# A second copy that writes over its source tile, weight sums in three instructions, and PSUM tiles of two banks in a two-layer encoder

## The chip, the cores and the metric

The kernel runs on one core of one Trainium2 chip. The metric is device microseconds of one execution. Three runs of the kernel before took 2028.54, 2030.12 and 2031.21 us, median 2030.12 us. Engines are called as the profile calls them: PE (matrix products), PEld (its weight loads), DVE (vector engine), ACT (scalar engine), POOL and SP (SP issues most DMAs).

## The reference

A two-layer encoder over 256 tokens of width 2048, all in float32. Layer 0 mixes tokens by chunked spatial gating, layer 1 by grouped-query attention; both also attend to 256 memory tokens. Each layer ends with a SwiGLU feed-forward, the part that the change touches most (`D_FF` is 5632).

```python
def swiglu(h, w_gate_up, w_down):
    gate, up = jnp.split(h @ w_gate_up, 2, axis=-1)
    return (jax.nn.silu(gate) * up) @ w_down

def reference(x, mem, g_mix, g_ffn, w_in_a, g_v_a, w_spatial, b_spatial, w_in_b, g_q_b, g_k_b,
              g_mem, w_mem_kv, g_mq, g_mk, w_out, w_gate_up, w_down):
    for l in range(DEPTH):
        h = rms_norm(x, g_mix[l])
        if l % N_MIXERS == 0:
            z = h @ w_in_a[ia]
            tok_in, q_mem = jnp.split(z, [2 * TOK_WIDTH], axis=-1)
            tok_out = chunked_spatial_gating(tok_in, g_v_a[ia], w_spatial[ia], b_spatial[ia])
        else:
            z = h @ w_in_b[ib]
            tok_in, q_mem = jnp.split(z, [TOK_WIDTH + 2 * KV_WIDTH], axis=-1)
            tok_out = gqa_axial_attention(tok_in, g_q_b[ib], g_k_b[ib], cos, sin)
        mem_out = memory_attention(q_mem, mem, g_mem[l], w_mem_kv[l], g_mq[l], g_mk[l])
        x = x + jnp.concatenate([tok_out, mem_out], axis=-1) @ w_out[l]
        x = x + swiglu(rms_norm(x, g_ffn[l]), w_gate_up[l], w_down[l])
    return x
```

(Lines that set indices and tables are left out.)

## The kernel before, in words

**Products.** A float32 operand is split into `hi` (rounded to the PE's fp32r type by ACT) and `lo` (the rest, by DVE). A product is three matmuls, hi·hi, lo·hi and hi·lo (`matmul3`, L197 to L201). Tokens stand on two partition blocks t = 0, 1 of 128 rows. Weights come by SP's DMAs into `raw` tiles of four 128x512 blocks; `halves` (L263) makes `whi` on ACT (L269) and `wlo` on DVE (L270), each in a ring of three buffers (`W_TILES`).

**The feed-forward.** Eleven gate/up blocks f of 512 columns go in three chunks (0 to 3, 4 to 7, 8 to 10). For each f a `Pair` (L325) computes a gate block and an up block for both t; `Silu` and a multiply give the activation `a` (L803 to L805, a ring `sg` of two buffers). Behind each chunk two `Pair`s (jj = 0, 1 in the code) multiply the chunk's activations with `w_down` and add into the residual tiles `X`. A `Pair` walks over items i, each two 128-row blocks of the weights. Slow items (`eight`) are 8 products, 24 matmuls, into four PSUM banks named 2, 3, 4, 8 (pool `psa`, printed as `acc`). Fast items (`seven`) are a seven-product scheme, 21 matmuls: sums of weight blocks (`T`, L361 to L365), sums of activations (`activation_sums`), the outer products 2, 3, 4 in `acc` banks and four inner products 1, 5, 6, 7 in banks of the pool `psm` (printed as `m`, four tiles of one bank). After the last fast item `inner` (L409) combines the four inner banks into four `e` tiles; in the down projection these are then added into X (L420); `outer` (L428) adds the outer banks at the end of the Pair.

**Turning the activations.** The down projection needs the activations with features on partitions. `turned` (L207) does it in steps: ACT copies the 16-bit planes of `a` apart into a tile `planes` (L212), a DMA on ACT's queue turns them into `back` (L213), and ACT copies them together again (L216), in the kernel before into the tile of `planes`. Then `split_a` (L785) splits the result: hi by ACT (L193), lo by DVE (L194); for two f of chunks 0 and 1 it makes the activation sums too.

**Buffers.** All these tiles (planes, back, hi, lo, sums) come from `big()` (L76): one tag `a` in the stage's pool `room["p"]`, with 26 buffers in a feed-forward stage (`FFN_TILES`) and 36 in a mixing stage. A tile's buffer is free when its last reader is done; an instruction that writes a new tile waits for a free buffer.

**What sets the order.** The program emits work in ticks: `later(n, f)` runs f when n more half-items have been emitted. The order of the instructions on each engine is then made by a planner (`schedule_with_timeline_sim=True`, L863), which simulates the program and takes, on each engine, the earliest emitted instruction that its simulation holds ready; an instruction that waits for a buffer in the simulation is passed over. On the chip each engine runs its list in order. How many `a` tiles live at once in a chunk's down projection follows from `fast` and `quick` (each listed item keeps a hi and a lo tile of activation sums, those of `fast` until the layer's last gate/up Pair) and from `split_a` (a hi and a lo tile for each f and t, kept for the chunk):

```python
FFN_TILES = 26
...
        fast = (0, 1, 2)
...
            quick = [2 * f + 1 for f in chunk[:2 if chunk[-1] < 10 else l]]
...
                    later(3 + t if f == chunk[-1] else 12 + t, lambda a=a, t=t, f=f: turn_a(a, t, f))
```

Of the kernel before, what the change touches and what calls it, by code (L numbers as in the profile page):

```python
# [17 lines left out]
P = 128  # L18
# [36 lines left out]
def encoder(ctx: ExitStack, tc: tile.TileContext, x, mem, g_mix, g_ffn, w_in_a, g_v_a, w_spatial, b_spatial,  # L55
# [11 lines left out]
    psm = ctx.enter_context(tc.tile_pool(name="psm", bufs=4, space=PS))  # L67
# [13 lines left out]

    def misc():
        return psm.tile([P, NB], F32, tag="m", name=nm("m"))
# [37 lines left out]
    X = [[xp.tile([P, NB], F32, name=f"x_{t}_{j}") for j in range(4)] for t in range(NT)]  # L121
# [10 lines left out]
    def gain_columns(kind):  # L132
        gcol[kind] = const.tile([P, 32], F32, name=f"gcol_{kind}")
        gps = misc()
# [72 lines left out]
    def turned(src, ticks, then):  # L207
# [7 lines left out]
        def finish():  # L215
            nc.scalar.copy(planes.rearrange("p (n h) -> p n h", h=2), back.rearrange("p (h n) -> p n h", h=2))  # L216
            then(a)
# [106 lines left out]

    class Pair:  # L325
# [5 lines left out]
        def __init__(self, parts, sums, w, na, nb, order, fast, into=None):  # L331
            self.parts, self.sums, self.w, self.na, self.nb, self.into = parts, sums, w, na, nb, into
            self.bank, self.part, self.ready = {}, {}, {}
# [20 lines left out]
        def prepare(self, i):  # L354
# [5 lines left out]
            if i in self.fast:  # L360
                T = room["p"].tile([P, KC3, NB], F32, tag="T", name=nm("T"), bufs=2)  # L361
                nc.vector.tensor_tensor(raw[:, 0], raw[:, 0], raw[:, 1], ALU.add)  # L362
                nc.vector.tensor_tensor(T[:, 0], raw[:, 0], raw[:, 3], ALU.add)
                nc.vector.tensor_tensor(T[:, 1], T[:, 0], raw[:, 1], ALU.subtract)
                nc.vector.tensor_tensor(T[:, 2], T[:, 0], raw[:, 2], ALU.add)  # L365
                self.ready[i] = raw, T
# [15 lines left out]
        def seven(self, i, raw, T):  # L382
            t1, w00, w10, w11 = halves(raw, KC4)
            t2, t3, t4 = halves(T, KC3)
# [23 lines left out]
        def inner(self):  # L408

            b, o = self.bank, self.into  # L410
            e, v, f, y = [room["p"].tile([P, NB], F32, tag=f"e{i}", name=nm("e"), bufs=1) for i in range(4)]
# [455 lines left out]
```

## Time and profile before

| | |
|---|---|
| median of three runs | 2030.12 us (2028.54 to 2031.21) |
| the profiled execution's own time | 2030.63 us |
| its span, first to last instruction | 2028.8 us, so 1.8 us lie around it |
| granted PE clock over the span | 0.998 |
| PE busy | 2006.1 us, 99% |
| PEld / DVE / ACT busy | 82% / 79% / 60% |
| first matmul, last matmul's end, from the span's start | 4.7 us, 2024.3 us |

How to read it: the page gives busy time by engine, then the chain of work that ended last, then groups of instructions by source line with the mean duration and the idle time in front of them. A timeline row is start, duration, engine, line, operation, output<-inputs, form, count, and in brackets how long the engine had been idle and which instruction ended the wait. A row of a stretch gives its length, then busy time and the number of instructions in brackets for each engine, then the granted PE clock, the DMA share and GB/s. Matmuls are pipelined: each is shown 0.39 us long, but the next one starts after about 0.23 us, so time that PE lost is read from counts of matmuls and not from its busy time.

### The profile page before, as it was taken

To read this page: it belongs to the slowest core of one execution; us is meant where nothing else is said; L and a number is where in the kernel's file an instruction comes from. 1 tells how busy PE (TensorE), PEld (TensorE's weight loads), DVE (VectorE), ACT (ScalarE), POOL (GpSimd) and SP (SyncE) were. 2 spreads that over 40 slices of the span, in tenths; PEclk is the share of its full clock that TensorE was granted. 3 is DMA by queue.
4 is the path that set the end of the run, shared out by engine and by line. 5 is a ranking of instruction groups with operands and counts; after the bars stand their busy time and mean duration, and the time that the engine had idled before them with its cause. 6 is when DMAs were issued, how large, how long until landed. Compare 5 with 4: busy or idle time off the path is not lost.

```text
span 2028.8 us, 24312 instructions
## 1 busy us (share of the span) xinstructions
PE 2006.1 (99%) x9058; PEld 1656.6 (82%) x9058; DVE 1603.5 (79%) x1862; ACT 1213.8 (60%) x1509; POOL 50.5 (2%) x80
## 2 busy tenths in 40 slices
PE   8999999999999999999999999999999999999999
PEld 7888888888788887888888888888887888878887
DVE  5576558998889988798666886599987899878977
ACT  7765476666445664456756765756654467634662
POOL 2010000000000000000010100000000000000000
PEclk9999999999999999999999999999999999999999
DMA  9754575666656666577766444756765566755564
GB/s 331 246 183 150 184 218 170 233 198 209 212 184 234 191 214 206 188 231 220 227 203 207 157 144 145 218 187 206 239 218 187 186 203 219 226 188 202 193 212 145
DMA packets 265791, 411.79 MB, mean 203 GB/s; under 512 B 74428, under 2 KB 74792, under 8 KB 265672
## 3 DMA queue, kind: packets, MB, share of 16 engines
q1 hardware_dynamic: 198800, 385.79, 56.3%
q10 hardware_dynamic: 64824, 18.02, 4.8%
q0 software_dynamic: 2048, 6.42, 1.0%
q8 instruction: 71, 1.16, 0.2%
q14 instruction: 48, 0.39, 0.1%
HBM read 390.26 MB, written 4.19 MB: 194 GB/s over the span
## 4 chain that ended last, share of the span: by engine, by line
PE 92%; DVE 3%; DMA 3%; ACT 1%; issue 1%; SPq 0%; DVEq 0%; ACTq 0%
PE acc L201 26%; PE acc L200 26%; PE acc L199 26%; PE m L201 4%; PE m L199 4%; PE m L200 4%; DMA a<-a 2%; DVE wlo L270 2%; ACT whi L269 1%; PE m L205 1%; PE m L515 0%; DMA x<-in_x 0%; PE m L661 0%; DVE T L365 0%; DMA raw<-in_w_in_a 0%
## 5 line engine op out<-in xcount | busy, mean ns | idle before, releaser
L270 DVE TENSOR_TENSOR wlo<-raw,whi 128x2048 fp32r<-128x2048 f32 (+2 forms) x465 | 839.0, 1826 | 242.8 <-ACT whi L269 235.8
L269 ACT CAST whi<-raw 128x2048 fp32r<-128x2048 f32 (+2 forms) x465 | 702.1, 1537 | 459.7 <-PE acc L200 376.5
L199 PE MATMUL acc<-whi,h 128*128 128x512 f32 x1440 | 562.6, 391 | 0.4 <-ACT whi L269 0.4
L200 PE MATMUL acc<-whi,h 128*128 128x512 f32 x1440 | 561.9, 390 | 0.0
L201 PE MATMUL acc<-wlo,h 128*128 128x512 f32 x1440 | 518.2, 391 | 0.8 <-DVE wlo L270 0.8
L199 PE MATMUL acc<-whi,a 128*128 128x512 f32 x1062 | 413.8, 392 | 2.5 <-DVE x L428 1.4
L200 PE MATMUL acc<-whi,a 128*128 128x512 f32 x1062 | 415.6, 391 | 0.0
L201 PE MATMUL acc<-wlo,a 128*128 128x512 f32 x1062 | 400.6, 391 | 0.8 <-DVE wlo L270 0.8
L201 PEld LDWEIGHTS acc<-wlo,h 128*128 128x128 f32 x1440 | 270.6, 188 | 56.9 <-DVE wlo L270 1.4
L199 PEld LDWEIGHTS acc<-whi,h 128*128 128x128 f32 x1440 | 270.6, 188 | 55.5 <-ACT whi L269 0.8
L200 PEld LDWEIGHTS acc<-whi,h 128*128 128x128 f32 x1440 | 270.6, 188 | 55.4
L199 PEld LDWEIGHTS acc<-whi,a 128*128 128x128 f32 x1062 | 199.7, 188 | 46.5 <-DVE x L428 3.0
L201 PEld LDWEIGHTS acc<-wlo,a 128*128 128x128 f32 x1062 | 200.2, 188 | 43.9 <-DVE wlo L270 2.7
L200 PEld LDWEIGHTS acc<-whi,a 128*128 128x128 f32 x1062 | 200.3, 189 | 41.3 <-DVE a L194 0.6
L269 ACT CAST whi<-T 128x1536 fp32r<-128x1536 f32 x82 | 121.4, 1481 | 132.9 <-PE acc L200 99.1
L270 DVE TENSOR_TENSOR wlo<-T,whi 128x1536 fp32r<-128x1536 f32 x82 | 143.9, 1755 | 20.7 <-ACT whi L269 20.7
L199 PE MATMUL m<-whi,a 128*128 128x512 f32 x264 | 103.5, 392 | 5.7 <-ACT whi L269 5.7
L200 PE MATMUL m<-whi,a 128*128 128x512 f32 x264 | 102.8, 390 | 0.0
L216 ACT COPY a<-a 128x1024 uint16<-128x1024 uint16 x60 | 70.2, 1170 | 37.3 <-DMA a<-a 37.1
L201 PE MATMUL m<-wlo,a 128*128 128x512 f32 x264 | 88.7, 395 | 2.4 <-DVE wlo L270 2.4
L362 DVE TENSOR_TENSOR raw<-raw 128x512 f32<-128x512 f32 x82 | 56.5, 688 | 22.8 <-DMA raw<-in_w_gate_up 22.8
L199 PEld LDWEIGHTS m<-whi,a 128*128 128x128 f32 x264 | 49.6, 188 | 18.4 <-ACT whi L269 8.3
(131 smaller groups left out, 1520.0 us busy)
## 6 DMA issues: line engine op xcount, KB each, us to landing
raw<-in_w_gate_up SPq DMA_DIRECT2D x352, 512.0 KB, 4.4
raw<-in_w_down SPq DMA_DIRECT2D x176, 512.0 KB, 5.1
raw<-in_w_out SPq DMA_DIRECT2D x32, 1024.0 KB, 5.2
raw<-in_w_in_a SPq DMA_DIRECT2D x24, 1024.0 KB, 5.1
raw<-in_w_in_b SPq DMA_DIRECT2D x24, 1024.0 KB, 5.0
raw<-in_w_mem_kv SPq DMA_DIRECT2D x16, 1024.0 KB, 5.0
raw<-in_w_in_a SPq DMA_DIRECT2D x7, 512.0 KB, 6.1
x<-in_x SPq DMA_DIRECT2D x8, 256.0 KB, 5.7
```

The source lines that it names most:

```text
L199: nc.tensor.matmul(out, lhsT=a[0], rhs=b[0], start=start, stop=False)
L200: nc.tensor.matmul(out, lhsT=a[1], rhs=b[0], start=False, stop=False)
L201: nc.tensor.matmul(out, lhsT=a[0], rhs=b[1], start=False, stop=stop)
L205: nc.tensor.transpose(dst[:, c * P:(c + 1) * P], src[:, c * P:(c + 1) * P], ident)
L216: nc.scalar.copy(planes.rearrange("p (n h) -> p n h", h=2), back.rearrange("p (h n) -> p n h", h=2))
L269: nc.scalar.copy(hi[:, cut], raw[:, cut])
L270: nc.vector.tensor_tensor(lo[:, cut], raw[:, cut], hi[:, cut].bitcast(F32), ALU.subtract)
L362: nc.vector.tensor_tensor(raw[:, 0], raw[:, 0], raw[:, 1], ALU.add)
```

## The change

Three edits, and what goes with them:

- `turned` gets a flag `over`, set for the feed-forward's activations: the second copy (L216) writes the joined words into the source tile (`sg`) instead of the tile of `planes`, and `split_a` reads them there.
- The weight sums of a fast item are three DVE instructions instead of four, one of them 128x1024; the first two results change places (`raw[:, 0]` and `T[:, 0]`), and with them which product reads which tile.
- The inner banks become two PSUM tiles of two banks, (1, 6) and (5, 7), from a pool that is opened for each stage (`open_rooms`). `inner` then takes three DVE instructions instead of four, and the addition into X three instead of four, with the four `e` tiles made one and X stored in tiles of two blocks. In a fast item that is not a Pair's first, product 6 moves to the front group and product 5 to the rear group. A lone `misc()` tile in a feed-forward stage takes a two-bank tile.

```diff
-    psm = ctx.enter_context(tc.tile_pool(name="psm", bufs=4, space=PS))
+    def open_rooms(scope, name, tiles, banks):
+
+        room["p"] = scope.enter_context(tc.tile_pool(name=name, bufs=tiles, reuse_waits="tile"))
+        room["m"] = scope.enter_context(tc.tile_pool(name=f"ps_{name}", bufs=4 // banks, space=PS))
+        room["banks"] = banks
+
+    def banks2():
+        return room["m"].tile([P, 2, NB], F32, tag="m", name=nm("m"))
+
     def misc():
-        return psm.tile([P, NB], F32, tag="m", name=nm("m"))
+        if room["banks"] == 2:
+            return banks2()[:, 0]
+        return room["m"].tile([P, NB], F32, tag="m", name=nm("m"))
...
-    def turned(src, ticks, then):
+    def turned(src, ticks, then, over=False):
...
         def finish():
-            nc.scalar.copy(planes.rearrange("p (n h) -> p n h", h=2), back.rearrange("p (h n) -> p n h", h=2))
-            then(a)
+            words = src.rearrange("p (c n) -> p c n", c=4) if over else a
+            halves = (src.bitcast(U16) if over else planes).rearrange("p (n h) -> p n h", h=2)
+            nc.scalar.copy(halves, back.rearrange("p (h n) -> p n h", h=2))
+            then(words)
...
-                nc.vector.tensor_tensor(raw[:, 0], raw[:, 0], raw[:, 1], ALU.add)
-                nc.vector.tensor_tensor(T[:, 0], raw[:, 0], raw[:, 3], ALU.add)
-                nc.vector.tensor_tensor(T[:, 1], T[:, 0], raw[:, 1], ALU.subtract)
-                nc.vector.tensor_tensor(T[:, 2], T[:, 0], raw[:, 2], ALU.add)
+                w01 = raw[:, 0].unsqueeze(1).to_broadcast([P, 2, NB])
+                nc.vector.tensor_tensor(T[:, :2], raw[:, 1:4:2], w01, ALU.add)
+                nc.vector.tensor_tensor(raw[:, 0], T[:, 0], raw[:, 3], ALU.add)
+                nc.vector.tensor_tensor(T[:, 2], raw[:, 0], raw[:, 2], ALU.add)
...
-                self.bank[name] = misc() if name in (1, 5, 6, 7) else psa.tile([P, NB], F32, tag="acc", name=nm("acc"))
-                self.part[name] = 0
+                if name in (1, 5, 6, 7):
+                    both = (1, 6) if name in (1, 6) else (5, 7)
+                    self.two[both] = banks2()
+                    self.bank.update({one: self.two[both][:, i] for i, one in enumerate(both)})
+                else:
+                    self.bank[name] = psa.tile([P, NB], F32, tag="acc", name=nm("acc"))
...
-            inner = [(1, get(k0, 0), w00), (5, q5, t1), (6, s2, t2), (7, q7, t3)]
+            inner = [(1, get(k0, 0), w00), (6, s2, t2), (5, q5, t1), (7, q7, t3)]
             outer = [(2, get(k1, 0), w10), (3, q3, w11), (4, get(k1, 1), t4)]
             if self.bank:
-                inner, outer = inner[:1] + outer[:2], inner[1:] + outer[2:]
+                inner, outer = inner[:2] + outer[:2], inner[2:] + outer[2:]
...
-            nc.scalar.copy(e, b[1])
-            nc.vector.tensor_tensor(v, b[6], e, ALU.subtract)
-            nc.vector.tensor_tensor(f, b[5], v, ALU.add)
-            nc.vector.tensor_tensor(v, b[7], v, ALU.add)
-            nc.vector.tensor_tensor(y, b[7], f, ALU.add)
+            nc.scalar.copy(E[:, 0], b[1])
+            nc.vector.tensor_tensor(E[:, 3], b[6], E[:, 0], ALU.subtract)
+            nc.vector.tensor_tensor(E[:, 1:3], self.two[5, 7], E[:, 3:].to_broadcast([P, 2, NB]), ALU.add)
+            nc.vector.tensor_tensor(E[:, 3], b[5], E[:, 2], ALU.add)
...
+            if t:
+                nc.vector.tensor_tensor(o[0], o[0], E[:, 2], ALU.subtract)
+                nc.vector.tensor_tensor(o[1], o[1], E[:, 3], ALU.add)
+            else:
+                nc.vector.tensor_tensor(o.whole, o.whole, E[:, :2], ALU.add)
...
-                turned(a, 2, lambda whole: split_a(whole, t, f, aT, aS, half, quick))
+                turned(a, 2, lambda whole: split_a(whole, t, f, aT, aS, half, quick), True)
```

More of the change, by code (lines that the diff above doesn't have):

```diff
@@ L119, in encoder @@
     nc.gpsimd.memset(mhalf, -0.5)
-    X = [[xp.tile([P, NB], F32, name=f"x_{t}_{j}") for j in range(4)] for t in range(NT)]
+    X2 = [[xp.tile([P, 2, NB], F32, name=f"x_{t}_{i}") for i in range(2)] for t in range(NT)]
+    X = [[X2[t][j // 2][:, j % 2] for j in range(4)] for t in range(NT)]
     def load_x(t, j):
@@ L133, in gain_columns @@
         gcol[kind] = const.tile([P, 32], F32, name=f"gcol_{kind}")
-        gps = misc()
+        gps = misc() if room else psa.tile([P, NB], F32, tag="acc", name=nm("acc"))
         nc.tensor.transpose(gps[:, :32], gst[kind], ident[:32, :32])
@@ L323, in activation_sums, with __init__ @@
         return [(hi[:, i, :], lo[:, i, :]) for i in range(4)]
+    class Columns(list):
+        def __init__(self, whole):
+            self.whole = whole
+            super().__init__(whole[:, n] for n in range(2))
     class Pair:
@@ L332, in __init__ @@
             self.parts, self.sums, self.w, self.na, self.nb, self.into = parts, sums, w, na, nb, into
-            self.bank, self.part, self.ready = {}, {}, {}
+            self.bank, self.two, self.part, self.ready = {}, {}, {}, {}
             self.order, self.fast = order, fast
@@ L408, in inner, with add_inner @@
         def inner(self):
-            b, o = self.bank, self.into
-            e, v, f, y = [room["p"].tile([P, NB], F32, tag=f"e{i}", name=nm("e"), bufs=1) for i in range(4)]
-            nc.scalar.copy(e, b[1])
-            nc.vector.tensor_tensor(v, b[6], e, ALU.subtract)
-            nc.vector.tensor_tensor(f, b[5], v, ALU.add)
-            nc.vector.tensor_tensor(v, b[7], v, ALU.add)
-            nc.vector.tensor_tensor(y, b[7], f, ALU.add)
-            if o:
-                for (t, n), x, op in (((0, 0), e, ALU.add), ((0, 1), f, ALU.add), ((1, 0), v, ALU.subtract),
-                                      ((1, 1), y, ALU.add)):
-                    later(1 + 2 * t + n, lambda o=o[t][n], x=x, op=op: nc.vector.tensor_tensor(o, o, x, op))
-            self.out = o or [[e, f], [v, y]]
+            b = self.bank
+            E = room["p"].tile([P, 4, NB], F32, tag="e", name=nm("e"), bufs=1)
+            nc.scalar.copy(E[:, 0], b[1])
+            nc.vector.tensor_tensor(E[:, 3], b[6], E[:, 0], ALU.subtract)
+            nc.vector.tensor_tensor(E[:, 1:3], self.two[5, 7], E[:, 3:].to_broadcast([P, 2, NB]), ALU.add)
+            nc.vector.tensor_tensor(E[:, 3], b[5], E[:, 2], ALU.add)
+            if self.into:
+                for t in range(NT):
+                    later(1 + t, lambda t=t: self.add_inner(E, t))
+            self.out = self.into or [[E[:, 2 * t + n] for n in range(2)] for t in range(NT)]
+        def add_inner(self, E, t):
+            o = self.into[t]
+            if t:
[3 more added lines that the diff above has]
+                nc.vector.tensor_tensor(o.whole, o.whole, E[:, :2], ALU.add)
         def outer(self, t):
@@ L624, in encoder @@
         scope = ExitStack()
-        room["p"] = scope.enter_context(tc.tile_pool(name=f"mix{l}", bufs=MIX_TILES, reuse_waits="tile"))
+        open_rooms(scope, f"mix{l}", MIX_TILES, 1)
         cat = Parts()
@@ L754, in encoder @@
             add_residual(linear(cat, w_out[l], j * NB, units), j, norm, gslice("ffn", l), hF, j < 3)
-        room.pop("p")
+        room.clear()
         scope.close()
         scope = ExitStack()
-        room["p"] = scope.enter_context(tc.tile_pool(name=f"ffn{l}", bufs=FFN_TILES, reuse_waits="tile"))
+        open_rooms(scope, f"ffn{l}", FFN_TILES, 2)
         sums = {}
@@ L814, in encoder @@
                     order.insert(2 * n + (2 if last else 0), i)
-                into = [[X[t][2 * jj + n] for n in range(2)] for t in range(NT)]
+                into = [Columns(X2[t][jj]) for t in range(NT)]
                 pairs.append(Pair(aT, aS, w_down[l], 2 * jj * NB, (2 * jj + 1) * NB, order, quick, into))
@@ L830, in encoder @@
         norm = next_norm
-        room.pop("p")
+        room.clear()
         scope.close()
```

5 lines of the change are left out of this document (3 added, 2 removed).

## The prediction

> **What bounds the kernel now.** I read the page first, then stretches of the trace, then the order of instructions in the stretches where PE lost time.
>
> ```profile
> span 2028.8 us, 24312 instructions
> ...
> PE 2006.1 (99%) x9058; PEld 1656.6 (82%) x9058; DVE 1603.5 (79%) x1862; ACT 1213.8 (60%) x1509; POOL 50.5 (2%) x80
> ...
> PE 92%; DVE 3%; DMA 3%; ACT 1%; issue 1%; SPq 0%; DVEq 0%; ACTq 0%
> ```
>
> PE is the bound: 92% of the chain that ends last is PE. No edit removes a matmul, so a gain can only come from time in which PE lacks work. DVE work that is saved elsewhere is worth nothing. The next rows are stretches of the trace: length, PE busy time with the number of matmuls, the other engines, the granted PE clock. The last four rows list PE alone.
>
> ```profile
> 410.00:480.00 70.00, 70.00 (x310) 57.83 (x309) 64.58 (x62) 47.91 (x39) 0.00 (x0) 1.00 0.71 228
> 526.00:536.00 10.00, 7.88 (x31) 5.34 (x31) 4.67 (x6) 1.93 (x2) 0.00 (x0) 1.00 0.31 108
> 780.00:790.00 10.00, 7.44 (x30) 5.01 (x29) 5.45 (x7) 1.47 (x1) 0.00 (x0) 1.00 0.37 124
> 1529.00:1540.00 11.00, 9.07 (x31) 6.45 (x30) 3.70 (x5) 2.54 (x2) 0.00 (x0) 0.84 0.28 95
> 1784.00:1796.00 12.00, 9.49 (x33) 6.77 (x32) 4.70 (x6) 2.53 (x2) 0.00 (x0) 0.86 0.27 89
> ...
> 495.00:526.00 31.00, 30.32 (x133) 1.00 0.77 246
> 750.00:780.00 30.00, 29.73 (x130) 1.00 0.79 247
> 1498.00:1529.00 31.00, 30.24 (x133) 1.00 0.75 239
> 1755.00:1784.00 29.00, 28.81 (x126) 1.00 0.76 247
> ```
>
> The first row is gate/up work: 70 us for 310 matmuls, 0.226 us each, PE never idle although DVE is busy 92% of it. At that pace the four short stretches lose 10 - 31 x 0.226 = 3.0, 10 - 30 x 0.226 = 3.2, 11 - 31 x 0.226 = 4.0 and 12 - 33 x 0.226 = 4.5 us: 14.7 us. (Counts include about one matmul that straddles the edge, so the true loss is up to 0.2 us larger in each.) The four rows ahead of them lose 0.9, 0.6, 0.9 and 0.5 us: 3.0 us. All eight lie in the down projections of chunks 0 and 1 of both layers. Two knots, an early and a late one, come four times.
>
> **The late knot.** The timeline of the first one:
>
> ```profile
> 505.38 0.68 DVE L194 TENSOR_TENSOR a<-a,a 128x512 fp32r<-128x512 f32 x1
> ...
> 508.54 0.63 ACT L193 CAST a<-a 128x512 fp32r<-128x512 f32 x1
> ...
> 529.24 1.47 ACT L269 CAST whi<-T 128x1536 fp32r<-128x1536 f32 x1 [7.14 <-PE acc L200]
> 530.75 1.76 DVE L270 TENSOR_TENSOR wlo<-T,whi 128x1536 fp32r<-128x1536 f32 x1 [2.43 <-ACT whi L269]
> 530.77 0.50 PE L199 MATMUL m<-whi,a 128*128 128x512 f32 x1 [1.33 <-ACT whi L269]
> 532.42 0.69 DVE L194 TENSOR_TENSOR a<-a,a 128x512 fp32r<-128x512 f32 x1
> 532.56 0.73 PE L201 MATMUL m<-wlo,a 128*128 128x512 f32 x2 [0.60 <-DVE wlo L270]
> ...
> 787.18 0.68 DVE L194 TENSOR_TENSOR a<-a,a 128x512 fp32r<-128x512 f32 x1
> ...
> 1534.44 0.68 DVE L194 TENSOR_TENSOR a<-a,a 128x512 fp32r<-128x512 f32 x1
> ...
> 1790.45 0.69 DVE L194 TENSOR_TENSOR a<-a,a 128x512 fp32r<-128x512 f32 x1
> ```
>
> L193 and L194 are hi and lo of the chunk's last activation, t = 0 first (L194 at 505.38) and then t = 1. For t = 1 hi is made at 508.54 but lo only at 532.42, 24 us later, behind the `wlo` of the next Pair. Without that lo the t = 1 products of the last f cannot run, so PE takes products of the next Pair early, until those need a third `whi` buffer, which the unfinished items still hold: ACT's cast waits 7.14 us for a PE release, PE waits 1.33 us for it and 0.60 us for `wlo`. The same L194 is late at 787.18, 1534.44 and 1790.45.
>
> Why is lo late? I count `a` tiles. When it is due there live: 6 of `fast` sums (3 x hi, lo), 4 of `quick` sums, 12 of the first three f (x 2 t x hi, lo), hi and lo of t = 0, hi of t = 1, and the `planes` tile that the split of t = 1 reads: 26, the whole pool. The lo would be the 27th. It must wait until the next Pair's first fast item has used up a `quick` sum. That is the order seen.
>
> **The change part by part.**
>
> (1) *Second copy over the source.* The words then stand in `sg`, `planes` is free once the DMA has read it, and the count is 6 + 4 + 12 + 4 = 26: lo fits. L194 can follow L193, near 509. From the early knot at 503 PE still has three slow items of other f ahead of the last f, 503 + 72 x 0.226 = 519, so lo has 10 us of room, and the instruction only moves forward on DVE. The late knots go: -14.7 us. The copy itself is the same 128x1024 copy. What it makes later is the release of `sg`:
>
> ```profile
> 395.33 0.68 DVE L194 TENSOR_TENSOR a<-a,a 128x512 fp32r<-128x512 f32 x1
> 401.42 0.72 ACT L804 ACTIVATE sg<-e,s 128x512 f32<-128x512 f32 x1 [0.78 <-DVE e L428]
> ```
>
> The last split of one f ends at 396.0 and the next f's first `sg` write is at 401.4: 5.4 us of cover, so 0. If it were gone, L804 would wait, and behind it on ACT the casts L269.
>
> By the rows the granted clock is 0.84 and 0.86 in the two late knots of layer 1 alone, and 1.00 beside them; I take it to return with PE's idle time. The Trainium skill, page "TensorE: Matmul & The Clock Gate", section "Part 1: The HAM clock gate", has the clock fall only after about 3.4 us of idle. The gaps shown are 1.33 and 0.60 us, so by the page the fall is not theirs and would stay: by an estimate 11 x 0.16 + 12 x 0.14 = 3.4 us less gain. No row here shows an idle stretch as long as the page wants.
>
> (2) *Merged DVE instructions.* The rows for their price:
>
> ```profile
> L270 DVE TENSOR_TENSOR wlo<-raw,whi 128x1024 fp32r<-128x1024 f32 x199 | 235.9, 1222 | 118.6 <-ACT whi L269 112.3 <-PE acc L201 5.1 <-PE m L205 0.7
> L362 DVE TENSOR_TENSOR raw<-raw 128x512 f32<-128x512 f32 x82 | 56.5, 688 | 22.8 <-DMA raw<-in_w_gate_up 22.8
> L420 DVE TENSOR_TENSOR x<-x,e 128x512 f32<-128x512 f32 x40 | 26.5, 686 | 0.0
> L416 DVE TENSOR_TENSOR e<-m,e 128x512 f32<-128x512 f32 x32 | 21.9, 685 | 0.0
> L663 DVE TENSOR_TENSOR a<-m,bcol 128x512 f32<-128x512 f32 x6 | 4.0, 690 | 0.5 <-PE m L661 0.4
> ```
>
> One 128x1024 for two 128x512 saves 2 x 688 - 1222 = 154 ns. A broadcast operand costs nothing (L663, 690 ns). An operand over two banks has no row; the bounds are 1222 and 2 x 685 ns, and I take 1222, the row of its size. There are 82 + 32 + 10 = 124 merges, 19 us of DVE, and PE never waits for DVE in the first stretch: 0. In the knots some DVE work is on the chain, 0 to -2 us.
>
> The cast of `raw` now waits for two weight sums, 1222 + 690 ns, instead of one of 688: 1.22 us later at most.
>
> ```profile
> ACT whi L269 <- PE acc L200: 475.6, 192, 7.6
> ...
> ACT a L216 <- DMA a<-a: 37.1, 21, 3.6
> ...
> ACT whi L269 <- DVE T L365: 28.4, 8, 3.6
> ```
>
> The casts wait 475.6 us for PE, 2.5 us a time over 192, so the sums have lead: 0. With that cover gone each late microsecond would reach PE through the `whi` ring.
>
> (3) *Two-bank tiles.* A Pair's products 5 and 7 wait until the last `inner` instruction has read (5, 7). The tightest place is f = 0 to f = 1:
>
> ```profile
> 361.23 0.69 DVE L416 TENSOR_TENSOR e<-m,e 128x512 f32<-128x512 f32 x1
> ...
> 362.89 0.39 PE L199 MATMUL m<-whi,a 128*128 128x512 f32 x1
> ```
>
> L416 ends at 361.9, 1 us before the next Pair's second inner product; product 5 moves behind 6, so 0, bound +1 us in each layer. The regrouping itself keeps four products from the `raw` halves (1, 6, 2, 3, before 1, 2, 3, 5) ahead of three from the `T` halves, so the `whi` ring turns as before. The new thing is at the feed-forward's start, where the two `norm_piece` tiles take both two-bank tiles:
>
> ```profile
> 336.34 0.39 PE L199 MATMUL m<-whi,h 128*128 128x512 f32 x1
> ...
> 338.38 0.39 PE L199 MATMUL m<-whi,a 128*128 128x512 f32 x1
> ...
> 340.46 0.35 DVE L242 SCALAR_TENSOR_TENSOR h<-m,gcol_ffn,h 128x128 fp32r<-128x128 f32 x1
> ```
>
> The inner products start at 336.34 and 338.38 in banks that were free; the norm pieces are read until 340.81. Now one product must wait up to 340.8 - 338.4 = 2.4 us, unless PE is given other matmuls, of which the next slow item has 24. Bounds 0 and +2.4 us a layer; I take 0.5 each, +1 us, nearer to 0 because the planner knows of this wait.
>
> (4) *Pools by stage.* The old stage's banks must be free before the new stage's first use:
>
> ```profile
> 240.32 0.69 DVE L194 TENSOR_TENSOR a<-m,a 128x512 fp32r<-128x512 f32 x1
> ...
> 322.93 0.60 PE L205 MATMUL m<-ident,x 128*128 128x128 f32 x4
> ```
>
> Last read 241.0, next use 322.9: 82 us of cover, so 0.
>
> Sum against the profiled execution (2030.63 us, span 2028.8 and 1.8 around it): 2030.63 - 14.7 + 1.0 = 2016.9; the median of the runs is 0.5 lower, so 2016.4 us, -0.7%.
>
> **The rivals.**
>
> *Early knot too.* Near 503 the second copy holds ACT while the turning DMA is under way (L216 waits 37.1 us for it in 21 places, up to 3.6 us), and the casts queued behind it are late. If the planner's new order puts casts ahead, 3.0 us more go and DVE's savings count: about 2012. Against: nothing in the change speeds the DMA or moves it.
>
> *New knots.* The planner lays all instructions anew; a late instruction elsewhere, or the two-bank wait at its full 2 x 2.4, gives back half: about 2024.
>
> *It does not free the tile in time.* If my count misses one live tile, lo stays the 27th: 2030, no change. For it: the count comes from the code, and no row names buffers. Against: hi of t = 1 got its buffer by 508.54 and lo did not, so the pool was short by exactly one then.
>
> *Slower.* The cast of `raw` behind two sums: if the planner puts a `wlo` (2.29 us for a 128x2048) between them, each of 82 fast items is late. It outweighs the gain from 14 / 82 = 0.17 us per item that reaches PE; a 1.22 us delay of which a third shows, 0.4 x 82 = 33, gives 2050. Against: in the first stretch, fast items among it, PE lost nothing with DVE at 92%.
>
> **How the numbers follow.** Forecast 0.56, early knot too 0.12, new knots 0.15, no change 0.10, slower 0.07. 0.2% is 4 us, about what a measurement of this kernel tells from no change. Faster: 0.56 + 0.12 + most of 0.15 = 0.82; same 0.11; slower 0.07. The likeliest case alone runs from 2013 (late knots at 0.2 us more each, DVE's 2 us) to 2021 (two-bank wait in full). The range takes in the early knot and most of the new knots: 2010 to 2026.
>
> **What would show it.** Right: L194 of t = 1 within some 5 us of its L193 in all four chunks; 10 us after 526 with about 44 matmuls; clock 1.00 in layer 1's down projections; PE's matmul count unchanged; L362's successor at 1.2 us. Wrong: L194 still behind the next Pair's `wlo<-T`; PE waiting for `h L242` near 338; casts L269 waiting for a weight sum; L804 waiting for L194.

## The result, and the profile after

The changed kernel takes 2011.05 us (median of 4 runs, 2010.67 to 2011.51), the kernel before 2030.66 us beside it (4 runs). The ratio is 0.9905, 95% interval 0.9888 to 0.9922: faster by about 1%. The profiled execution took 2011.51 us with a span of 2009.7 us, 19.1 us less than the one of before. Forecast were 2016.4 us and a range of 2010 to 2026: the time lies in the range, 5.4 us below the forecast.

Lines move by the change: L193/L194 (hi and lo) are now L204/L205, the products L199 to L201 are L210 to L212, the turn's two copies and its DMA L212/L216 and L213 are L223/L229 and L224, the weight's hi and lo L269/L270 are L282/L283, the gate's multiply L805 is L835.

From the page of the changed kernel, span, engines and the chain that ended last:

```profile
span 2009.7 us, 24209 instructions
...
PE 1998.0 (99%) x9058; PEld 1655.5 (82%) x9058; DVE 1595.0 (79%) x1738; ACT 1218.4 (61%) x1509; POOL 58.2 (3%) x80
...
PE 98%; DMA 1%; DVE 0%; ACT 0%; SPq 0%; issue 0%; ACTq 0%; DVEq 0%
```

The matmuls are the same 9058. The chain is 98% PE, before 92%: what was lost to DVE, DMA and ACT on it is gone. DVE has 124 instructions fewer (1862 to 1738), as counted, but only 8.5 us less busy time.

The stretches of the prediction, now in the changed kernel (length, PE busy, PEld, DVE, ACT, POOL, granted clock, DMA share, GB/s):

```profile
495.00:526.00 31.00, 31.00 (x138) 25.69 (x137) 25.90 (x20) 18.48 (x14) 0.00 (x0) 1.00 0.72 226
526.00:536.00 10.00, 10.00 (x45) 8.29 (x45) 8.22 (x10) 4.01 (x4) 0.00 (x0) 1.00 0.44 144
750.00:780.00 30.00, 29.78 (x132) 24.14 (x131) 23.82 (x21) 14.22 (x10) 0.00 (x0) 1.00 0.69 211
780.00:790.00 10.00, 10.00 (x46) 8.29 (x45) 8.83 (x8) 5.22 (x3) 0.00 (x0) 1.00 0.57 192
1498.00:1529.00 31.00, 31.00 (x139) 25.57 (x138) 27.68 (x25) 16.30 (x12) 0.00 (x0) 1.00 0.59 199
1529.00:1540.00 11.00, 11.00 (x50) 9.13 (x49) 8.01 (x4) 6.97 (x5) 0.00 (x0) 1.00 0.71 228
1755.00:1784.00 29.00, 29.00 (x130) 24.02 (x129) 26.58 (x24) 10.89 (x7) 0.00 (x0) 1.00 0.65 215
1784.00:1796.00 12.00, 12.00 (x55) 9.94 (x54) 9.48 (x7) 7.70 (x5) 0.00 (x0) 1.00 0.76 261
```

Where PE had 31, 30, 31 and 33 matmuls in the four late knots it has 45, 46, 50 and 55, and it is never idle. The early stretches are nearly full as well: 138, 132, 139 and 130 matmuls for 133, 130, 133 and 126, with 0.22 us of idle left in the second. The clock is 1.00 in all of them.

The timeline of the changed kernel shows hi and lo of the last activation, t = 1, in the first chunk of the first layer:

```profile
509.02 0.62 ACT L204 CAST a<-sg 128x512 fp32r<-128x512 f32 x1
...
511.87 0.69 DVE L205 TENSOR_TENSOR a<-sg,a 128x512 fp32r<-128x512 f32 x1
```

The lo follows its hi after 2.9 us; it was 24 us. In the other three chunks it is the same 2.9 us (lo at 763.68, 1505.14 and 1755.22). This is the event on which the prediction rested.

### The profile page after: what moved, and what is told of

It is laid out like the page before. It is cut to its first block, busy times and chain, and to the rows that moved or that the text cites. A ratio compares the mean times of both kernels' runs of the same rounds, so it can differ in the third digit from the quotient of the medians.

```text
span 2009.7 us, 24209 instructions
## 1 busy us (share of the span) xinstructions
PE 1998.0 (99%) x9058; PEld 1655.5 (82%) x9058; DVE 1595.0 (79%) x1738; ACT 1218.4 (61%) x1509; POOL 58.2 (3%) x80
## 3 DMA queue, kind: packets, MB, share of 16 engines
q8 instruction: 71, 1.16, 0.2%
## 4 chain that ended last, share of the span: by engine, by line
PE 98%; DMA 1%; DVE 0%; ACT 0%; SPq 0%; issue 0%; ACTq 0%; DVEq 0%
PE acc L212 28%; PE acc L211 28%; PE acc L210 28%; PE m L212 4%; PE m L210 4%; PE m L211 4%; PE m L216 1%; DVE wlo L283 0%; PE m L545 0%; DMA x<-in_x 0%; DMA a<-a 0%; PE m L691 0%; DMA raw<-in_w_in_a 0%; ACT whi L282 0%; ACT sg L229 0%
## 5 line engine op out<-in xcount | busy, mean ns | idle before, releaser
L283 DVE TENSOR_TENSOR wlo<-raw,whi 128x2048 fp32r<-128x2048 f32 (+2 forms) x465 | 841.8, 1826 | 262.2 <-ACT whi L282 237.3
L282 ACT CAST whi<-raw 128x2048 fp32r<-128x2048 f32 (+2 forms) x465 | 707.1, 1541 | 453.8 <-PE acc L211 370.9
L210 PE MATMUL acc<-whi,h 128*128 128x512 f32 x1440 | 562.6, 391 | 0.0
L212 PE MATMUL acc<-wlo,h 128*128 128x512 f32 x1440 | 518.0, 391 | 0.7 <-DVE wlo L283 0.6
L210 PE MATMUL acc<-whi,a 128*128 128x512 f32 x1062 | 413.4, 390 | 0.0
L212 PE MATMUL acc<-wlo,a 128*128 128x512 f32 x1062 | 398.8, 390 | 0.2 <-DVE wlo L283 0.2
L212 PEld LDWEIGHTS acc<-wlo,h 128*128 128x128 f32 x1440 | 270.5, 188 | 58.3 <-DVE wlo L283 3.1
L210 PEld LDWEIGHTS acc<-whi,h 128*128 128x128 f32 x1440 | 270.6, 188 | 55.5 <-ACT whi L282 0.8
L212 PEld LDWEIGHTS acc<-wlo,a 128*128 128x128 f32 x1062 | 199.4, 188 | 42.1 <-DVE wlo L283 0.9
L210 PEld LDWEIGHTS acc<-whi,a 128*128 128x128 f32 x1062 | 199.4, 188 | 41.0 <-ACT whi L282 0.2
L282 ACT CAST whi<-T 128x1536 fp32r<-128x1536 f32 x82 | 121.7, 1484 | 106.5 <-PE acc L211 98.6
L283 DVE TENSOR_TENSOR wlo<-T,whi 128x1536 fp32r<-128x1536 f32 x82 | 143.9, 1755 | 10.5 <-ACT whi L282 10.5
L381 DVE TENSOR_TENSOR T<-raw 128x1024 f32<-128x1024 f32 x82 | 100.2, 1222 | 22.5 <-DMA raw<-in_w_gate_up 21.6
L210 PE MATMUL m<-whi,a 128*128 128x512 f32 x264 | 102.7, 389 | 0.0
L212 PE MATMUL m<-wlo,a 128*128 128x512 f32 x264 | 102.7, 389 | 0.0
L229 ACT COPY sg<-a 128x1024 uint16<-128x1024 uint16 x44 | 51.6, 1173 | 36.7 <-DMA a<-a 35.0
L458 DVE TENSOR_TENSOR e<-acc,e 128x512 f32<-128x512 f32 x88 | 58.4, 690 | 2.6 <-PE acc L212 2.6
```

What stands on the lines that cost most here:

```text
L210: nc.tensor.matmul(out, lhsT=a[0], rhs=b[0], start=start, stop=False)
L212: nc.tensor.matmul(out, lhsT=a[0], rhs=b[1], start=False, stop=stop)
L229: nc.scalar.copy(halves, back.rearrange("p (h n) -> p n h", h=2))
L282: nc.scalar.copy(hi[:, cut], raw[:, cut])
L283: nc.vector.tensor_tensor(lo[:, cut], raw[:, cut], hi[:, cut].bitcast(F32), ALU.subtract)
L381: nc.vector.tensor_tensor(T[:, :2], raw[:, 1:4:2], w01, ALU.add)
```

## The experiments

The theory has two parts. **Part one**: the pool of `a` tiles is one buffer short for the last lo, and this alone makes the late knots. **Part two**: the weight sums in three instructions and the two-bank tiles cost or bring next to nothing. The rivals to part one: another cause that the new order happens to cure. To part two: the other edits bring the rest of the gain by themselves, or cost something that the whole hides.

What the changed kernel consists of is called *over* (second copy over the source), *sums* (weight sums in three instructions, the products regrouped with them) and *banks* (two-bank tiles, `inner`, merged additions).

### e1_over: the kernel before with over alone

```
-                turned(a, 2, lambda whole: split_a(whole, t, f, aT, aS, half, quick))
+                turned(a, 2, lambda whole: split_a(whole, t, f, aT, aS, half, quick), True)
```

(with the `over` branch in `turned`)

> The kernel before with the second copy over its source tile alone; weight sums, banks and additions as before. Theory 1 (one buffer short): the late knot comes from the 27th live `a` tile, and this edit alone frees it, so the split's lo of the chunk's last activation follows its hi within 5 us in all four chunks and the four late stretches lose nothing: 2030.4 - 14.7 = about 2015.5. Rival (a lucky new order): the gain comes from the merged DVE instructions that let the planner lay the work anew; this kernel then keeps the late knots, about 2030. For the early knot: if merged DVE instructions removed it, it stays here (2015 to 2016); if the freed buffer did, it goes (2011 to 2012).

Measured: 2014.91 us against 2031.84, ratio 0.9919 (0.9905 to 0.9934). Four stretches that hold the late knots with their tails, PE alone, first in the kernel before, with one longer stretch from the start of the feed-forward that is used further below:

```profile
526.00:545.00 19.00, 16.88 (x71) 1.00 0.36 121
780.00:800.00 20.00, 17.44 (x74) 1.00 0.38 127
1529.00:1548.00 19.00, 17.07 (x66) 0.91 0.33 111
1784.00:1803.00 19.00, 16.49 (x64) 0.91 0.28 92
...
330.00:500.00 170.00, 169.70 (x747) 1.00 0.63 205
```

The same four in e1_over:

```profile
526.00:545.00 19.00, 19.00 (x86) 1.00 0.56 182
780.00:800.00 20.00, 20.00 (x90) 1.00 0.52 164
1529.00:1548.00 19.00, 19.00 (x85) 1.00 0.53 168
1784.00:1803.00 19.00, 19.00 (x86) 1.00 0.72 238
```

275 matmuls became 347 in the same 77 us: 72 more, at 77 / 347 = 0.222 us each 16.0 us. The time fell by 16.9 us. So over alone brings the late knots' whole price and, within the interval, nothing else.

### e4_lo_in_sg: the kernel before, the one lo from another ring

Over is not in this kernel. Only the lo that is late, t = 1 of the last f of chunks 0 and 1, takes its tile from the `sg` ring instead of the pool.

```
-                hi, lo = split(whole, [P, 4, P])
+                if t == NT - 1 and f in (3, 7):
+                    hi = big(F32R, [P, 4, P])
+                    lo = kp.tile([P, 4, P], F32R, tag="sg", name=nm("sg"), bufs=2)
+                    nc.scalar.copy(hi, whole)
+                    nc.vector.tensor_tensor(lo, whole, hi.bitcast(F32), ALU.subtract)
+                else:
+                    hi, lo = split(whole, [P, 4, P])
```

> The kernel before with one edit of another kind: the lo tile of the last activation's second token block of chunks 0 and 1 is taken from the ring of the activations (`sg`) and not from the pool; the second copy still goes into the tile of the planes. It too saves one pool buffer where it lacks. Theory 1 (one buffer short): late knots gone, 2014 to 2017. Rival (it is the place that the second copy writes to, or the new order, that counts): 2029 to 2031.

Measured: 2015.86 us, ratio 0.9925 (0.9910 to 0.9940). The four stretches hold 86, 90, 85 and 86 matmuls, as in e1_over; the first of them:

```profile
526.00:545.00 19.00, 19.00 (x86) 1.00 0.52 167
```

A wholly different edit, with nothing in common but one pool tile less at that moment, gives the same gain. The missing buffer is the cause of the late knots.

### e2_no_over and e3_pool25: the changed kernel with the buffer taken away again

e2_no_over leaves the last argument of the call away:

```
-                turned(a, 2, lambda whole: split_a(whole, t, f, aT, aS, half, quick), True)
+                turned(a, 2, lambda whole: split_a(whole, t, f, aT, aS, half, quick))
```

> The changed kernel without the second copy over its source: it goes back into the tile of the planes. Weight sums, banks and additions as changed. Theory 1 (one buffer short): the late knots are all back, with lo over 15 us behind its hi, and with the clock under 1.00 in layer 1's two; the early knot stays away if the DVE edits removed it: 2011.1 + 14.7 to 2011.1 + 18, so 2026 to 2029. Rival (new order): no late knot, 2011 to 2013.

e3_pool25 keeps over and makes the pool one tile smaller (`FFN_TILES` 26 to 25).

> The changed kernel with 25 instead of 26 buffers in the feed-forward's pool, nothing else. Theory 1 (count of live tiles): 26 tiles are needed at the split's lo, so with 25 the same late knot is back in all four chunks: 2024 to 2030. Rival (new order, the pool was never the limit): 2011 to 2013.

Measured: 2052.5 us (ratio 1.0099, 1.0077 to 1.0120) and 2053.4 us (1.0118, 1.0089 to 1.0147). The knots are back in both, larger than before. The timeline of e2_no_over around the first one:

```profile
529.92 0.50 PE L212 MATMUL m<-wlo,a 128*128 128x512 f32 x1 [1.74 <-DVE wlo L283]
...
535.24 1.76 DVE L283 TENSOR_TENSOR wlo<-T,whi 128x1536 fp32r<-128x1536 f32 x1 [3.58 <-ACT whi L282]
...
538.58 0.69 DVE L205 TENSOR_TENSOR a<-a,a 128x512 fp32r<-128x512 f32 x1 [1.58 <-PE m L211]
```

and its stretch, PE alone:

```profile
526.00:545.00 19.00, 14.64 (x48) 0.82 0.33 109
```

The same stretch in e3_pool25:

```profile
526.00:545.00 19.00, 16.05 (x69) 1.00 0.27 88
```

The lo L205 stands again behind the `wlo<-T` of the next Pair, waiting for PE to release its tile, 26 us behind its hi (512.16), and one tile fewer does the same without any change in the turn: hi at 509.29 and lo at 536.31 in e3_pool25. Both are 20 us slower than the kernel *before*, though. By part two of the theory the knots alone should have come back, and with them about the time of before (2026 to 2029 and 2024 to 2030 were expected). This was the first sign against part two: without the buffer, sums and banks together cost 20 us.

Most of these 20 us lie at the knots. The stretches 500 to 560, 740 to 830, 1500 to 1560 and 1750 to 1830 us, which hold the knots, have 1196 matmuls in the kernel before, 1130 in e2 and 1119 in e3: 66 and 77 fewer, 15 and 17 us at 0.226 us, of 22.6 and 17.7 us between the profiled executions. In both the lo of t = 0 now waits too: DVE stands at it for 2.47 us in e2 (508.20) and for 5.12 us in e3 (504.24), and in the kernel before (505.38) not at all.

### e5 to e8: sums and banks, alone and with over

e5_over_sums is e1_over with

```
-                nc.vector.tensor_tensor(raw[:, 0], raw[:, 0], raw[:, 1], ALU.add)
-                nc.vector.tensor_tensor(T[:, 0], raw[:, 0], raw[:, 3], ALU.add)
-                nc.vector.tensor_tensor(T[:, 1], T[:, 0], raw[:, 1], ALU.subtract)
-                nc.vector.tensor_tensor(T[:, 2], T[:, 0], raw[:, 2], ALU.add)
+                w01 = raw[:, 0].unsqueeze(1).to_broadcast([P, 2, NB])
+                nc.vector.tensor_tensor(T[:, :2], raw[:, 1:4:2], w01, ALU.add)
+                nc.vector.tensor_tensor(raw[:, 0], T[:, 0], raw[:, 3], ALU.add)
+                nc.vector.tensor_tensor(T[:, 2], raw[:, 0], raw[:, 2], ALU.add)
...
-            t1, w00, w10, w11 = halves(raw, KC4)
-            t2, t3, t4 = halves(T, KC3)
+            t2, w00, w10, w11 = halves(raw, KC4)
+            t1, t3, t4 = halves(T, KC3)
```

and the old order of the products.

> The kernel before with two of the three edits: the second copy over its source and the weight sums in three instructions; inner banks as four tiles of one bank, inner and additions as before. If the weight sums take away the early knot (fewer DVE instructions ahead of the activation's multiply, so the turn's first copy and its DMA come earlier), about 2012 and no PE loss near 503; if the two-bank tiles or the merged inner instructions do it, about 2015.5 with 3 us lost near 503, 758, 1506 and 1761 together.

e6_over_banks is e1_over with the rest of the change: `banks2`, the pairs (1, 6) and (5, 7), the new order of the products, the new `inner` and `add_inner`, and the four old weight sums.

> The kernel before with the other two edits: the second copy over its source, the two-bank tiles with merged inner and additions; weight sums in four instructions as before. If the weight sums take away the early knot, it stays here: about 2015.5. If the two-bank edit does it, about 2012. The wait for the norm pieces' two-bank tiles at the start of each feed-forward costs 0 to 2.4 us a layer here as in the changed kernel.

e7_sums is the kernel before with the weight sums and the new order of the products, in four single banks and without over. e8_banks is e6_over_banks without over.

> The kernel before with the weight sums in three instructions and with the changed order of the products 6 and 5; second copy and banks as before. Theory 1 (one buffer short): late knots stay, so 2027 (if the early knot goes) to 2030. Rival (new order): 2011 to 2016.

> The kernel before with the two-bank tiles, merged inner and additions, and the changed order of the products; second copy and weight sums as before. Theory 1 (one buffer short): late knots stay, 2027 to 2031, and at most 5 us more where the norm pieces hold both tiles. Rival (new order): 2011 to 2016.

Measured, each against the kernel before on the same chip:

| over | sums | banks | kernel | median us | ratio (95%) |
|---|---|---|---|---|---|
| yes | no | no | e1_over | 2014.91 | 0.9919 (0.9905 to 0.9934) |
| no | yes | no | e7_sums | 2037.31 | 1.0030 (1.0018 to 1.0043) |
| no | no | yes | e8_banks | 2051.3 | 1.0100 (1.0085 to 1.0115) |
| yes | yes | no | e5_over_sums | 2028.01 | 0.9982 (0.9967 to 0.9997) |
| yes | no | yes | e6_over_banks | 2035.77 | 1.0023 (1.0013 to 1.0034) |
| no | yes | yes | e2_no_over | 2052.5 | 1.0099 (1.0077 to 1.0120) |
| yes | yes | yes | the change | 2011.05 | 0.9905 (0.9888 to 0.9922) |

Three pairs differ by over alone: the kernel before and e1, e8 and e6, e2 and the change. It gains 17, 16 and 41 us. Beside over, sums and banks are each a loss without the other (e5 and e6 lie 13 and 21 us above e1), and together a gain of 4 us (e1's runs lie at 2014.3 to 2017.3 us, the change's at 2010.7 to 2011.5). None of the four came where it was expected: e5 and e6 at 2012 or 2015.5, e7 at 2027 to 2030, e8 at no more than 2036. The three parts do not add up, so what sums or banks "are worth" can't be read from a kernel that has one of them. Where does e6 lose? The late knots are gone in e5 and e6 (85 and 86 matmuls in the first stretch). Long stretches, PE alone, show it. In e6_over_banks:

```profile
330.00:500.00 170.00, 163.50 (x713) 1.00 0.62 195
...
1310.00:1500.00 190.00, 183.10 (x796) 0.99 0.64 196
```

In the changed kernel:

```profile
330.00:500.00 170.00, 169.94 (x750) 1.00 0.65 205
...
1310.00:1500.00 190.00, 189.96 (x842) 1.00 0.66 210
```

PE is idle for 6.5 and 6.9 us there in e6, for 0.06 and 0.04 in the changed kernel and for 0.3 us in the first stretch of the kernel before. Most of e6's loss is in the gate/up work of the first chunk of each layer, where the change as a whole loses nothing.

The same two stretches in the other kernels tell which parts make this loss. The first has 747 matmuls in e1, e5 and e7, and 742 and 750 in e2 and e3; it has 713 in e8, as in e6. The second has 826 to 839 in the former and 802 in e8. So the loss comes where banks stand beside the old weight sums, with over or without it, and stays away where both are changed or banks are not. In e6 PE's waits in the two stretches, 6.5 and 6.8 us, are all for a cast (`whi`) or its lo (`wlo`) and none for a PSUM tile; so are those in e8. e5 loses in other places, and no stretch stands out: 12 matmuls fewer than the changed kernel from 500 to 560 us, 9 from 560 to 740, 9 from 1750 to 1830. Its ten runs lie between 2021.5 and 2033.1 us, the profiled one at 2022.9, so its profile shows only part of its loss.

### e9, e10 and e11: the second copy one tick later

In e6_over_banks several of the new gaps come right behind an ACT that stands at the second copy of the turn until the turning DMA has landed; the casts of weights queue behind it. One number, the tick at which that copy is due, was changed in three kernels: e6_over_banks (e9_over_banks_t3), the changed kernel (e10_after_t3) and e1_over (e11_over_t3).

```
-                turned(a, 2, lambda whole: split_a(whole, t, f, aT, aS, half, quick), True)
+                turned(a, 3, lambda whole: split_a(whole, t, f, aT, aS, half, quick), True)
```

> The kernel of e6_over_banks with one number changed: the second copy of the turn is due three ticks after its DMA is issued, not two. Theory (the losses of e6 come mostly from ACT standing at that copy until the turning DMA has landed, with the weight casts queued behind it): ACT's wait for the DMA (42.5 us in 18 places in e6) falls below 20 us, the 15 us of PE time lost within 6 us behind such waits go, and the time is about 2020 (2015 to 2025). Rival (e6 is slow because its order as a whole was laid badly, and the waits at the copy are only beside it): ACT's wait may fall, but the time stays at 2031 to 2040. A second rival, that every new order scatters by some 10 us whatever the cause, would show as a time that does not follow the wait.

> The changed kernel with the same one number (three ticks for two). There ACT waits 35.0 us in 16 places at the second copy, but only 1.4 us of PE's lost time lies behind such waits. Theory (the copy's wait is the cause of the early losses, and the change has already lost them): 2009.5 to 2012, no difference from the changed kernel's 2011. Rival (scatter of the order): anything from 2011 to 2035.

> The kernel before with the second copy over its source (e1_over, 2014.9) and three ticks for two. The early losses of e1 near 500, 750, 1500 and 1750 (about 3.7 us together) stand behind ACT's wait for the turning DMA. Theory: they go, 2011 to 2012, as the changed kernel. Rival (the early losses are not the DMA's, or come back elsewhere): 2014 to 2016, or more if the order scatters.

Measured: 2028.93 us (0.9994, 0.9985 to 1.0004), 2012.27 us (0.9915, 0.9900 to 0.9930) and 2014.95 us (0.9929, 0.9914 to 0.9944). e9 gained 7 us on e6 but stayed short of the 2015 to 2025 that the theory wanted; e10 and e11 moved by nothing that can be told from zero. The edit was a weak one: it did not take the wait away. At that copy ACT waits for the DMA 38.5 us in all in e9 (42.5 in e6; below 20 was expected), and the one at 464.00 waits 4.16 us where it waited 3.36 in e6. A later due time doesn't move the copy far, because the planner orders the instructions anew. In e11 the theory (2011 to 2012) failed, and its rival (2014 to 2016) came: the early losses stay, and ACT's wait at the copy is 27.3 us for 24.7. For e6 the test neither confirms nor refutes the wait as the main cause.

### e12_banks_order: the products' order apart from the banks

The change alters the place of the sums and the order of the products together. (In the kernel before, product 5 already opened the rear group of a fast item that is not a Pair's first, so there the new order moves product 6 alone to the front.) With the old sums and the new order (e6, e8) product 6 takes its weights from the sum tile early while 5 still needs the raw tile late, so two cast buffers are held through an item; with the new sums and the old order (e5) it is the other way round. e12 is e6_over_banks with the old order.

```
-            inner = [(1, get(k0, 0), w00), (6, s2, t2), (5, q5, t1), (7, q7, t3)]
+            inner = [(1, get(k0, 0), w00), (5, q5, t1), (6, s2, t2), (7, q7, t3)]
...
-                inner, outer = inner[:2] + outer[:2], inner[2:] + outer[2:]
+                inner, outer = inner[:1] + outer[:2], inner[1:] + outer[2:]
```

> The kernel of e6_over_banks with one thing put back: a fast item's products come in the order of the kernel before (1, 2, 3, then 5, 6, 7, 4). With the old weight sums the operands of 1, 2, 3, 5 lie in the raw tile and those of 6, 7, 4 in the sum tile; in e6 the order was 1, 6, 2, 3, 5, 7, 4, so that product 6 needs the sum tile's cast early while 5 still holds the raw tile's cast: two of the three cast buffers are held through the whole item. Theory (e6, e8 and, the other way round, e5 were slow because the order of the products and the place of the sums, which the change alters together, were taken apart there; the two-bank tiles and the merged additions themselves cost nothing): 2010 to 2016, and the losses of e6 near 350, 420, 460 and 1430 to 1480 are gone, its 3.6 us cast waits for a product 5 too. Rival 1 (the two-bank tiles cost PE time by themselves, 5 and 7 waiting for one tile): 2028 to 2036, as e6. Rival 2 (ACT's wait for the turning DMA makes e6's losses): about 2029 to 2036 as well, since the turn is the same as in e6. Rival 3 (scatter of the planner's order): anything between.

Measured: 2029.27 us, ratio 0.9998 (0.9988 to 1.0008), where 2010 to 2016 was expected. The torn pairing costs about 5 us of e6's 21 over e1 at most (1.0023 to 0.9998), and the gaps stay where they were. The time does not tell the first two rivals apart, which both had about 2028 to 2036. The waits speak against the first, that products wait for the two-bank tiles: in the two long stretches all of PE's waits are for a cast or its lo again. The first long stretch in e12_banks_order, PE alone:

```profile
330.00:500.00 170.00, 164.57 (x719) 1.00 0.59 195
```

What the gaps are can be read from the order of ACT. The timeline of e12_banks_order at two of them:

```profile
343.27 0.62 ACT L204 CAST a<-a 128x512 fp32r<-128x512 f32 x1 [4.18 <-DVE a L334]
345.30 1.91 ACT L282 CAST whi<-raw 128x2048 fp32r<-128x2048 f32 x1 [1.40 <-PE acc L211]
...
462.34 1.17 ACT L229 COPY sg<-a 128x1024 uint16<-128x1024 uint16 x1 [2.46 <-DMA a<-a]
...
463.71 1.90 ACT L282 CAST whi<-raw 128x2048 fp32r<-128x2048 f32 x1 [0.20 <-DMA raw<-in_w_gate_up]
...
465.66 0.50 PE L210 MATMUL acc<-whi,h 128*128 128x512 f32 x1 [1.37 <-ACT whi L282]
```

And the same two places in the changed kernel:

```profile
340.49 1.92 ACT L282 CAST whi<-raw 128x2048 fp32r<-128x2048 f32 x1 [0.75 <-ACT a L204]
...
456.90 1.92 ACT L282 CAST whi<-raw 128x2048 fp32r<-128x2048 f32 x1
...
458.72 1.16 ACT L229 COPY sg<-a 128x1024 uint16<-128x1024 uint16 x1
```

In e12 the cast of a weight stands behind an instruction that waits 4.18 us for DVE, or 2.46 us for a DMA; in the changed kernel the cast comes first. ACT's instructions and their durations are the same. At these two places, then, the loss goes with the order that the planner laid. In all four kernels with banks and the old sums (e6, e8, e9, e12) the first long stretch has only 711 to 719 matmuls, whatever the order of the products, the tick and over; so this is not a chance scatter of each new order. Why the planner lays that order with four sums and banks and not with three sums is **open**; so is whether every gap of e5 to e9 is of this kind, since only these places were read.

## Why the prediction was right, and where it was not

**Step 1, the late knot: right, in mechanism and nearly in size.** The count of 27 tiles for 26 buffers is confirmed from four sides: one buffer more by either of two edits removes the knots (e1, e4), one less by either of two brings them back (e2, e3). The term was -14.7 us; the windows of e1 give 16.0. In the prediction's own short stretches the changed kernel has 196 matmuls for 125, 71 more, 15.8 us at 0.222: the term was short by the matmul that straddles each stretch's edge, named there with 0.2 us a stretch and not added, and by little else. "It does not free the tile in time" is refuted.

**Step 1, the clock.** I took the clock of 0.84 and 0.86 to return with PE's idle time, and it did: 1.00 in all stretches. These two figures are means of a step. The kernel before, PE alone:

```profile
1534.50:1537.75 3.25, 3.18 (x8) 0.50 0.00 0
```

The clock is 1.00 up to 1534.25 and from 1538.00 on; about 1790.5 to 1793.9 looks the same. Half a clock for 3.4 us costs 1.7 us of work, so by this estimate the two steps are 3.4 of the 14.7 us. The PE waits ahead of each are 1.33 and 0.60 us, as in the first late knot, where the clock stayed at 1.00: what makes the difference is open. The prediction's estimate of 3.4 us for the clock was thus right in size. The Trainium skill, page "TensorE: Matmul & The Clock Gate", section "Part 1: The HAM clock gate", ties a fall to an idle window of about 3.4 us, by which 3.4 us of the gain would have stayed away. The measurement decides against that use of it. e2 says so once more: its clock of 0.82 is two such steps to 0.50, in a stretch whose longest PE wait is 1.74 us.

**Step 2, the merged instructions: right in price, wrong in what they are worth.** The groups of the changed kernel, by form (busy us and mean ns of one):

```profile
L381 DVE TENSOR_TENSOR T<-raw 128x1024 f32<-128x1024 f32 x82 | 100.2, 1222 | 22.5 <-DMA raw<-in_w_gate_up 21.6 <-DMA raw<-in_w_down 0.8
...
L437 DVE TENSOR_TENSOR e<-m,e 128x1024 f32<-128x1024 f32 x32 | 39.1, 1220 | 0.0
```

1222 ns with a broadcast operand and 1220 over two banks, as taken. The saving of 154 ns a merge was too large, though: 8.5 us over 124 are 69 ns. Two separate 128x512 start 0.60 us apart where nothing holds the second (488.41, 489.01 and 489.61 in the timeline of before below), so a pair takes 1.20 us to the next start and not 2 x 0.69; a merged one takes 1.14 us (1505.74 to 1506.88 in the changed kernel), 0.06 us less. The cast of `raw` does wait for the second weight sum now, 25.2 us in five places (L282 for L382, up to 5.4 us), but PE hardly loses by it: in the changed kernel it waits for a `whi` nowhere and for a `wlo` 0.8 us in all. "Slower" is refuted for this kernel. The failed step is the one that called the DVE edits 0 to -2 us, and with it the sentence on the early knot that "nothing in the change speeds the DMA or moves it". The rival "early knot too", about 2012 us, is what came; the prediction gave it 0.12. The first early knot in the timeline of the kernel before:

```profile
488.41 0.69 DVE L365 TENSOR_TENSOR T<-T,raw 128x512 f32<-128x512 f32 x1
...
489.01 0.69 DVE L428 TENSOR_TENSOR e<-acc,e 128x512 f32<-128x512 f32 x1
489.61 0.75 DVE L805 SCALAR_TENSOR_TENSOR sg<-e,s,sg 128x512 f32<-128x512 f32 x1
...
492.43 1.28 ACTq L213 DMA_TRANSPOSE a<-a  x1
...
499.42 1.17 ACT L216 COPY a<-a 128x1024 uint16<-128x1024 uint16 x1 [3.47 <-DMA a<-a]
499.42 1.25 ACTq L213 DMA_TRANSPOSE a<-a  x1
...
501.24 1.90 ACT L269 CAST whi<-raw 128x2048 fp32r<-128x2048 f32 x1
...
503.20 0.50 PE L199 MATMUL acc<-whi,a 128*128 128x512 f32 x1 [0.46 <-ACT whi L269]
503.37 1.17 ACT L216 COPY a<-a 128x1024 uint16<-128x1024 uint16 x1 [0.23 <-DMA a<-a]
```

and in the changed kernel:

```profile
486.15 0.69 DVE L383 TENSOR_TENSOR T<-raw 128x512 f32<-128x512 f32 x1
...
488.56 0.74 DVE L835 SCALAR_TENSOR_TENSOR sg<-e,s,sg 128x512 f32<-128x512 f32 x1
...
491.27 1.48 ACTq L224 DMA_TRANSPOSE a<-a  x1
...
497.01 1.18 ACT L229 COPY sg<-a 128x1024 uint16<-128x1024 uint16 x1
497.14 1.25 ACTq L224 DMA_TRANSPOSE a<-a  x1
...
498.96 1.91 ACT L282 CAST whi<-raw 128x2048 fp32r<-128x2048 f32 x1
503.85 1.17 ACT L229 COPY sg<-a 128x1024 uint16<-128x1024 uint16 x1 [2.98 <-DMA a<-a]
```

The gate's multiply, which the first copy and the DMA wait for, comes 1.05 us earlier, since one weight sum (L383) stands between the last `wlo` and it now where three stood (L363, L364, L365), the DMA comes 1.16 us earlier, and the second copy of t = 0 starts without a wait. From issue to the copy it is 6.99 us before and at most 5.74 now, so this transfer itself is quicker.

It is tempting to lay this on the load of the DMA engines. The DMA share from 495 to 500 us (it can pass 1, as it is counted) falls from 1.08 to 0.69. In the other three early knots of the kernel before, the first turn takes 6.62, 7.08 and 6.50 us from issue to copy at a share of 1.10 to 1.11 in the 5 us around the copy. But the second turn of the same pair, t = 1, speaks against it. In the changed kernel it takes 6.71 us (497.14 to 503.85) at a share of 0.76 over that time; before it took 3.95 us at 0.90. ACT stands 2.98 us for it now, and 4.37, 3.85 and 2.99 us at that turn in the other three chunks. Over the whole kernel ACT waits longer for turning DMAs than before: 47.5 us in 24 places, 37.1 us in 21 before.

So the waits did not go; they moved to where PE can bear them. Before, the long wait stands ahead of the cast at 501.24, and PE waits for a cast at 503.20. In the changed kernel a cast comes ahead of the long wait, at 498.96, and PE is not idle (31.00 of 31.00 us). A new order that puts casts ahead is what the rival named. This is read from rows: no run moved the cast, or made the transfer quicker, by itself, so what removes the early knot stays argued and not shown. The gain in the four early stretches: 138 + 132 + 139 + 130 matmuls for 133 + 130 + 133 + 126, 17 at 0.222 = 3.8 us. The four stretches of the late knots hold 347 matmuls here, as in e1, so their 16.0 us stand, and the sum closes: 2030.63 - 16.0 - 3.8 = 2010.8 against 2011.51 in the profiled execution.

**Step 3, two-bank tiles: +1.0 us forecast, none found.** The changed kernel has 750 matmuls from 330 to 500 us, the kernel before 747; PE doesn't wait for the norm pieces' tiles. The bound of zero was the right end, for banks beside sums.

**"New knots", given 0.15, did not come here** but in the kernels with over and only one of the other two parts (e5, e6, e9, e12) they took 13 to 21 us back, more than the half of the gain that I gave them. No step of the prediction told that the whole change would escape them: it costed each edit in the order of before, as if the planner would keep it. That the whole change escaped is luck as far as the prediction goes.

**Step 4** (pools by stage): cost nothing that can be seen, as costed; no run took it apart.

The likeliest case's own range, 2013 to 2021, missed the time; the full range held it because it reached to the early knot's rival.

## What to carry to other kernels

When an instruction runs long after its inputs are there, count the live tiles of its pool from the code: one buffer too few can show as waits of a quite different engine, and the proof is cheap, since any other edit that spares one tile must give the same gain. Where a planner lays the order, "one part of the change alone" also measures a new order; take parts out in several combinations before a part is given a price, and look for casts that stand behind a waiting instruction on an in-order engine. When a wait seems to vanish, add up all the waits of its kind over the kernel: here ACT's waits for the turning DMA grew from 37.1 to 47.5 us while PE's loss behind them went.

## What was not expected of the hardware

The clock fell in steps of one size, at short gaps. In the kernel before it went to 0.50 for 3.4 us, once in each late knot of layer 1, behind PE waits of 1.33 and 0.60 us; in e2's stretch of 19 us it did so twice (from 530.4 to 533.9 and from 537.3 to 540.7), with no single PE wait above 1.74 us and 4.4 us of idle in all (19.00 - 14.64), while e3's stretch with 2.95 us of idle kept 1.00. A mean of 0.82 to 0.86 over a stretch hides this. The turning DMA of one 128x512 tile took from about 4 to 8.4 us between issue and the copy behind it, and the DMA share of that time does not tell which: 3.95 us at 0.90 and 6.99 at 0.86 in the kernel before, 6.71 at 0.76 and 8.1 at 0.77 (747.56 to 755.65) in the changed one, 8.4 at 0.89 in e5 (492.60 to 500.99). And ACT is busy 1216.5 us in e6 and 1218.4 in the changed kernel, which is 25 us faster: what the queue does hardly changed, and at the places that were read the order of its casts had.
